# Mixer of a two-layer trunk: decay-weighted x made ahead of the scan, output transposes behind the next projection, B and C projected over all tokens at once

## The chip, the cores and the metric

The kernel runs on one core of a Trainium2 chip. The metric is the device time of one execution in microseconds (us); the kernel before has a median of 2000.05 us over three runs.

## The reference

Two layers, each of three sublayers on an x of 512 tokens by 1024 features, all in float32: a SwiGLU feed-forward, a mixer, a second feed-forward. Each sublayer reads a shifted and scaled x, its output is gated and added to x, and a layer norm follows. The change is in the mixer alone.

```python
h = modulate(x, shift, scale)
proj = h @ mix_w_in[l]                       # 1024 -> 3084
p_ssd, p_fox, p_sc = jnp.split(proj, ...)
y = jnp.concatenate([mamba2_group(p_ssd), fox_group(p_fox), shortconv_group(p_sc)]) @ mix_w_out[l]
x = layer_norm(ALPHA * x + gate * y)
```

The first group is a state space scan (SSD) with 8 heads of 64 features. Its projections are z, x, B and C; x, B and C go through a causal convolution of 4 taps and a SiLU. With dt a positive step for each token and head, a = -dt * A and cs the running sum of a inside a chunk, it computes

```python
y_diag = einsum(C B^T, exp(cs_i - cs_j), x * dt)         # inside a chunk
states = einsum(B, exp(cs_last - cs), x * dt)            # decay-weighted x: what a chunk leaves behind
y = y_diag + C @ (state carried in) * exp(cs) + D * x
y = rmsnorm(y * silu(z)) * norm_g                        # in two groups of 256 features
```

The second group is causal attention with a forgetting bias, 4 heads of 64, in four blocks of 128 queries (projections q, k, v). The third is B * conv3(C * x), from three projections of 256 features that the kernel calls SB, SC and SX.

## The kernel before

**Tiles.** The 512 tokens are four tiles of 128, one to a chunk of the scan (the kernel's chunk is 128 tokens) and one to a query block of the attention. The projections that the scan and the attention read by feature (B, C, x, q, k, SB, SC, SX) are made transposed: 128 features on the partitions, 512 tokens along the row. A call of feat (L761) makes 256 features, which are two PSUM banks of 128 features by 512 tokens.

**Exact products.** Each large product is three TensorE products (mm3): operands are split into a rounded high part and a remainder, and lo x hi, hi x lo and hi x hi are added up in PSUM. Names ending in h and l, or starting with them (hh, hl, hm, lm), are such pairs. Weights come by DMA from SyncE's queue in pieces of 128 x 2048; ScalarE makes the high part and VectorE subtracts it (the instructions named lm1z, lo, li and so on). The scan's small products, and the transposes with ident as the other operand, take plain float32.

**B and C.** feat has two switches for them. With halves=True a projection goes over tokens 0 to 255 for both banks and then over tokens 256 to 511, 8 k-steps of 3 products for each of the four quarters: 96 products 256 wide. All other calls of feat make 48 products 512 wide. With between=decays, the function decays (TensorE sums of a, the exponential edec, the attention's bias rows ncf) is called after the quarter that BPOS (L33) names, the third, and its first product is pinned behind that quarter's last one.

**The scan.** After x, B and C a loop over the four chunks transposes x back (pxt), and VectorE makes xdt = x * dt and xd = x * D from it. ssd_decay(i) makes the decay matrices: C B^T (pbc), masked by VectorE to cbm; the masked a (am, on GpSimd, L948), two TensorE products pd for each group, an exponential on ScalarE, and a VectorE product with cbm, which gives m. ssd_state(i) makes xw = xdt * edec in a temporary slot on VectorE, the products pss = B^T xw, and the new state. ssd_y(i) makes py = m xdt, eight products 64 wide, and adds it to xd; from chunk 1 on it adds the carried state's share. ssd_state is called for chunks 0 to 2 only, since nothing reads the state that the last chunk leaves. These steps stand between the projections of q, k and z.

**The end of the scan.** ssd_out(i) multiplies xd by the gate, takes the mean square of two groups with ScalarE, then a power of -1/2 on GpSimd (rs, L1001) and scales xd by it on VectorE (xd<-xd,rs). Then four TensorE transposes (pyt) turn the chunk to features by tokens; ScalarE evicts them with the norm's weight (yf) and makes the high part yh, and VectorE the remainder yl. These feed the output projection (po).

**The attention.** attn(i) makes qa, the split query, and then for each of four heads the scores (pS), their maximum (VectorE), the exponential (ScalarE), the scaled probabilities (prob), their transposes (pPT) and the products with the values (pfo).

**What sets the order.** The source is written in one order per step, and Tile's scheduler orders each engine's instructions from it by its own estimate; `after(ins, prev)` (it calls issue_after, L60) pins one instruction behind another on the same engine. Buffers come from pools: four PSUM banks in psa for projections, four in psb for everything else, 28 long-lived slots of 128 x 512 (slot), 9 temporary ones (tmp), 6 weight units. Engines are wrapped (InOrder, L43 to L56), so the profile gives L53 as the line of every recorded TensorE, VectorE and ScalarE instruction; which step it is can be read from its tile's name. At the end of the mixer the steps are called in the order attn(0), ssd_out(0), SC, attn(1), ssd_out(1), SX, attn(2), ssd_out(2), SB, attn(3), ssd_out(3), then the output projection.

Of the kernel before, what the change touches and what calls it, by code (L numbers as in the profile page):

```python
# [8 lines left out]
F32 = mybir.dt.float32  # L9
# [3 lines left out]
ALU = mybir.AluOpType  # L13
AX = mybir.AxisListType

P = 128
# [3 lines left out]
KD = D // P  # L20
# [9 lines left out]
NW = 6  # L30
PAD_W = 16
POS = 1
BPOS = 2  # L33
TICK = object()
CR = (2.7, 1.3)
WSZ = 1024
# [1 line left out]
C_Z, C_XS, C_B, C_C, C_DT = 0, 512, 1024, 1280, 1536  # L38
# [23 lines left out]
def issue_after(tc, ins, prev):  # L62

    tc.add_manual_dep(ins.ins, prev.ins.name,
                      mybir.DependencyInfo(mybir.DependencyClass.NoSync, mybir.DependencyReason.DATA),
                      reason="issue order")
# [3 lines left out]
def trunk(ctx, tc, x, c, ln_in_g, ln_in_b, ada_w, ada_b, ffn1_w_in, ffn1_w_out,  # L70
# [5 lines left out]
    pe, dve, act = (InOrder(tc, e) for e in (nc.tensor, nc.vector, nc.scalar))  # L76
# [18 lines left out]
    def pa(shape, name):  # L95
        return psa.tile(shape, F32, tag="a", name=name)

    def pb(shape, name):
        return psb.tile(shape, F32, tag="b", name=name)

    def slot(shape, dt, name):
        return lp.tile(shape, dt, tag="s", name=name)

    def tmp(shape, name, dt=F32):
        return tp.tile(shape, dt, tag="t", name=name)

    def mm3(ps, lh, ll, rh, rl, first, last):
        pe.matmul(ps, ll, rh, start=first, stop=False)
        pe.matmul(ps, lh, rl, start=False, stop=False)
        mm_last[0] = pe.matmul(ps, lh, rh, start=False, stop=last)  # L110

    mm_last = [None]

    def after(ins, prev):
        if prev is not None:
            issue_after(tc, ins, prev)


    ident = const.tile([P, P], F32, name="ident")
# [298 lines left out]
    def cols_unit(w, c0, name, prev=None):  # L418

        v = load(w, c0, 0, KD, 256, name)  # L420
        return [split(v[:, :, j * P:(j + 1) * P], f"{name}_{j}", prev) for j in range(2)]
# [6 lines left out]
    hT = [None, None]  # L428
# [203 lines left out]
    def x_affine(s, eng):  # L632

        ln_vectors(s)
        for t in range(NT):
            for h in range(2):
                xh = xt[t][:, h * 512:(h + 1) * 512]
                eng.tensor_tensor(xh, xh, aff[s, "g", h], ALU.mult)  # L638
                eng.tensor_tensor(xh, xh, aff[s, "b", h], ALU.add)
# [118 lines left out]
    def mixer(s, l):  # L758
        w_in, w_out = mix_w_in[l], mix_w_out[l]

        def feat(c0, name, epi, halves=False, between=None):  # L761

            us = cols_unit(w_in, c0, name)
            banks = [pa([P, T], f"pj{name}_{j}") for j in range(2)]
            for (a, b) in (((0, 256), (256, 512)) if halves else ((0, 512),)):
                for j in range(2):
                    wh, wl = us[j]
                    for k in range(KD):
                        mm3(banks[j][:, a:b], wh[:, k, :], wl[:, k, :],
                            hT[0][:, k, a:b], hT[1][:, k, a:b], k == 0, k == KD - 1)  # L770
                    if between is not None and (a > 0) * 2 + j == BPOS:
                        between(mm_last[0])
            for j in range(2):
                epi(j, banks[j])

# [2 lines left out]
        def conv_silu(ci, dst):  # L778
            def epi(j, ps):
                cc = ci + j  # L780
                w = lambda k: v_l[:, R_CW + k * 8 + cc:R_CW + k * 8 + cc + 1]
                acc = slot([P, T], F32, f"cv{s}_{cc}")
                act.activation(acc, ps, AF.Identity, scale=w(3), bias=v_l[:, R_CB + cc:R_CB + cc + 1])
                for sh in (1, 2, 3):
                    dve.scalar_tensor_tensor(acc[:, sh:], ps[:, :T - sh], w(3 - sh), acc[:, sh:],
                                             op0=ALU.mult, op1=ALU.add)
                silus.append(act.activation(acc, acc, AF.Silu))
                after(silus[-1], exp_done)
                dst[cc] = acc
            return epi  # L790

        xbc = {}
# [4 lines left out]
        us = []  # L797
# [8 lines left out]
        for t in range(NT):  # L806
            ts = slice(t * P, (t + 1) * P)
            ps = pa([P, 268], f"pv{s}_{t}")
            for k in range(KD):
                wh, wl = us[k // 3]  # L810
# [63 lines left out]
                dve.tensor_tensor(ncf[o:o + 4], psr[o:o + 4], ncf[o:o + 4].bitcast(F32), ALU.subtract)  # L874

        exp_done = edec = ncf = None
        feat(C_B, f"m{s}b", conv_silu(4, xbc), halves=True, between=decays)
        feat(C_C, f"m{s}c", conv_silu(6, xbc), halves=True)
        x_affine(s, pool)
        feat(C_XS, f"m{s}x0", conv_silu(0, xbc))  # L880
        feat(C_XS + 256, f"m{s}x1", conv_silu(2, xbc))
# [3 lines left out]
        for tt in range(2):  # L885
            ps = pb([P, 2, 2, P], f"pbt{s}_{tt}")
# [4 lines left out]
            b = slot([P, 2, 2, P], F32, f"btok{s}_{tt}")  # L891
# [1 line left out]
            btok.append(b)  # L893


        xdt, xd = [], []
        for t in range(NT):
            ts = slice(t * P, (t + 1) * P)
            ps = pb([P, 8, 64], f"pxt{s}_{t}")
            for cc in range(4):  # L900
                pe.transpose(ps[:, 2 * cc:2 * cc + 2, :], xbc[cc][:, ts], ident)
            if t % 2 == 0:
                xp = adap.tile([P, 2, 8, 64], F32, tag="ra", name=f"xdt{s}_{t}")
            a = xp[:, t % 2]
            b = slot([P, 8, 64], F32, f"xd{s}_{t}")
            dve.tensor_tensor(a, ps, dt8[:, t, :].unsqueeze(2).to_broadcast([P, 8, 64]), ALU.mult)
            dve.tensor_tensor(b, ps, dbc[l].unsqueeze(2).to_broadcast([P, 8, 64]), ALU.mult)
            xdt.append(a)
            xd.append(b)


        zs = []
# [45 lines left out]

        def ssd_state(i):

            xw = tmp([P, 8, 64], f"xw{s}_{i}")
            dve.tensor_tensor(xw, xdt[i], edec[:, 2, i, :].unsqueeze(2).to_broadcast([P, 8, 64]), ALU.mult)
            pss = pb([P, 8, 64], f"pss{s}_{i}")
            for g in range(2):
                pe.matmul(pss[:, 4 * g:4 * g + 4, :], btok[i // 2][:, i % 2, g, :],
                          xw[:, 4 * g:4 * g + 4, :], start=True, stop=True)
            snew = slot([P, 8, 64], F32, f"st{s}_{i}")
            if i == 0:
                act.activation(snew, pss, AF.Copy)
            else:  # L970
                dve.tensor_tensor(snew, state[i - 1], edec[:, 1, i, :].unsqueeze(2).to_broadcast([P, 8, 64]),
                                  ALU.mult)
                dve.tensor_tensor(snew, snew, pss, ALU.add)
            state.append(snew)
# [13 lines left out]
                dve.tensor_tensor(yo, pso, edec[:, 0, i, :].unsqueeze(2).to_broadcast([P, 8, 64]), ALU.mult)  # L988
                dve.tensor_tensor(xd[i], xd[i], yo, ALU.add)

        def ssd_out(i):
            y = xd[i].rearrange("p h d -> p (h d)")
            dve.tensor_tensor(y, y, zs[i], ALU.mult)
            ss = sm.tile([P, 2], F32, tag="ss", name="ss")
            sq = tmp([P, 512], "sq")
            for g in range(2):
                act.activation(sq[:, g * 256:(g + 1) * 256], y[:, g * 256:(g + 1) * 256], AF.Square,
                               scale=0.5, accum_out=ss[:, g:g + 1])
            dve.tensor_scalar(ss, ss, 1.0 / 256, RMS_EPS, op0=ALU.mult, op1=ALU.add)
            rs = sm.tile([P, 2], F32, tag="rs2", name="rs2")  # L1000
            pool.tensor_tensor(rs, ss, mhalf, ALU.pow)  # L1001
            for g in range(2):
                gs = slice(g * 256, (g + 1) * 256)
                dve.tensor_scalar(y[:, gs], y[:, gs], rs[:, g:g + 1], 0.5, op0=ALU.mult, op1=ALU.mult)
            ps = pb([P, 4, P], f"pyt{s}_{i}")
            for cc in range(4):
                pe.transpose(ps[:, cc, :], y[:, cc * P:(cc + 1) * P], ident)
            yf = slot([P, 4, P], F32, f"yf{s}_{i}")
            for cc in range(4):
                act.activation(yf[:, cc, :], ps[:, cc, :], AF.Copy, scale=v_l[:, R_NG + cc:R_NG + cc + 1])  # L1010
            yh = slot([P, 4, P], F32R, f"yh{s}_{i}")
            yl = slot([P, 4, P], F32R, f"yl{s}_{i}")
            act.activation(yh, yf, AF.Copy)
            dve.tensor_tensor(yl, yf, yh.bitcast(F32), ALU.subtract)
            yT.append((yh, yl))
# [110 lines left out]
        ssd_decay(0)  # L1126
        ssd_decay(1)
        ssd_state(0)
        ssd_y(0)
        feat(C_K, f"m{s}k", k_epi)  # L1130
        ssd_decay(2)
        ssd_state(1)
        ssd_y(1)
        z_proj()
        ssd_decay(3)
        ssd_state(2)
        ssd_y(2)
        ssd_y(3)
        attn(0)
        ssd_out(0)  # L1140
        feat(C_SC, f"m{s}sc", c_epi)
        attn(1)
        ssd_out(1)
        feat(C_SX, f"m{s}sx", x_epi)
        attn(2)
        ssd_out(2)
        feat(C_SB, f"m{s}sb", b_epi)
        attn(3)
        ssd_out(3)

        acts = [(lambda t, k=k: (yT[t][0][:, k, :], yT[t][1][:, k, :])) for k in range(4)]
        acts += [(lambda t, k=k: (fT[t][0][:, k, :], fT[t][1][:, k, :])) for k in range(2)]
# [6 lines left out]
    for s in range(6):  # L1159
        l, j = divmod(s, 3)  # L1160
# [39 lines left out]
```

## Time and profile before

| | us |
|---|---|
| median of three runs | 2000.05 |
| the three runs | 2003.78, 1996.82, 2000.05 |
| the profiled execution | 2000.76 |
| its span, first to last instruction | 1999.0 |
| mean granted TensorE clock | 0.995 |
| first mixer, from the B projection to the last attention block | about 416 to 616 |
| second mixer, the same stretch | about 1395 to 1595 |

The profiler took one execution. In its rows PE is TensorE's products, PEld its weight loads, DVE VectorE, ACT ScalarE, POOL GpSimd and SP SyncE. A row of the timeline gives start, duration, engine, line, operation, output<-inputs, shape and count; a bracket behind it is the engine's idle time just before, and the instruction that ended it. A row of the groups gives minimum/median/maximum or mean durations in ns and the first and last start. A row of the stages gives the stretch, its length, then each engine's busy time in the order PE, PEld, DVE, ACT, POOL, the granted clock, the DMA engines' busy share and GB/s. A row of the waits gives waiting tile, releasing tile, total us, count and longest. The second mixer's instructions lie about 979 us behind the first's and run in the same order.

### The profile page before, as it was taken

The numbers are of one execution on the slowest core, as the hardware profiler recorded it, in microseconds if no ns is written. First come the engines' busy times: TensorE is split into PE (matmuls) and PEld (weight loads), VectorE is DVE, ScalarE is ACT, GpSimd is POOL, SyncE is SP. The second block draws the span as 40 slices with busy tenths as digits, with TensorE's granted clock in tenths as the row PEclk, the third lists the DMA queues.
The fourth block names the chain that finished last, engine by engine and source line by source line (L and its number), as shares of the span: only waits on it lengthen the run. The fifth ranks groups of instructions, "written<-read, shape, count | busy, mean of one in ns | idle before, by whom it ended". The sixth has DMA issues, their size and how long they took to land.

```text
span 1999.0 us, 23434 instructions
## 1 busy us (share of the span) xinstructions
PE 1947.5 (97%) x9422; PEld 1627.3 (81%) x9422; DVE 1208.1 (60%) x1770; ACT 690.9 (35%) x1094; POOL 220.6 (11%) x182
## 2 busy tenths in 40 slices
PE   5999999999999999999999999999999999999998
PEld 4777878898878988888898788788978798888887
DVE  8886663477677655543477857435766785433336
ACT  3433223164365432123152322223544553222320
POOL 0230000007100040000005000000260004000000
PEclk9999999999999999999999999999999999999999
DMA  9766542234211544432345746232422144323331
GB/s 327 235 196 225 173 166 82 75 106 127 84 65 53 184 153 163 155 107 93 106 151 188 248 163 229 86 103 57 135 87 83 53 133 142 105 85 106 104 107 43
DMA packets 178605, 263.99 MB, mean 132 GB/s; under 512 B 9676, under 2 KB 124736, under 8 KB 178496
## 3 DMA queue, kind: packets, MB, share of 16 engines
q1 hardware_dynamic: 174000, 254.98, 38.8%
q10 hardware_dynamic: 4496, 7.52, 1.3%
q8 instruction: 74, 1.21, 0.2%
q14 instruction: 35, 0.29, 0.0%
HBM read 260.37 MB, written 2.10 MB: 131 GB/s over the span
## 4 chain that ended last, share of the span: by engine, by line
PE 77%; DVE 11%; DMA 7%; ACT 3%; issue 2%; POOL 0%; POOLq 0%; ACTq 0%; SPq 0%; DVEq 0%
PE pf L53 37%; PE po L53 23%; DMA ra<-in_ada_w_dram 6%; DVE acc L53 4%; PE pz L53 2%; DVE li L53 2%; DVE af L53 1%; PE pjm4x L53 1%; PE pjm1x L53 1%; PE ptr L53 1%; PE pS L53 1%; DMA ri<-in_ffn_w_in_dram 1%; PE py L53 1%; DVE x L53 1%; DVE gy L53 1%
## 5 line engine op out<-in xcount | busy, mean ns | idle before, releaser
L53 PE MATMUL pf<-hh,li 128*128 128x512 f32 (+1 forms) x1504 | 567.8, 378 | 1.4 <-DVE li L53 1.0
L53 PE MATMUL pf<-hl,hi 128*128 128x512 f32 (+1 forms) x1504 | 566.9, 377 | 0.2 <-DVE hl L53 0.2
L53 PE MATMUL pf<-hh,hi 128*128 128x512 f32 (+1 forms) x1504 | 566.9, 377 | 0.0
L53 DVE TENSOR_TENSOR li<-ri,hi 128x1024 fp32r<-128x1024 f32 x176 | 224.7, 1282 | 184.0 <-ACT hi L53 183.8
L53 PEld LDWEIGHTS pf<-hh,li 128*128 128x128 f32 x1504 | 284.4, 189 | 53.4 <-DVE li L53 1.7
L53 PEld LDWEIGHTS pf<-hl,hi 128*128 128x128 f32 x1504 | 284.2, 189 | 52.2 <-DVE hl L53 0.9
L53 PEld LDWEIGHTS pf<-hh,hi 128*128 128x128 f32 x1504 | 284.5, 189 | 51.3
L53 ACT ACTIVATE hi<-ri 128x1024 fp32r<-128x1024 f32 x176 | 185.5, 1060 | 311.1 <-PE pf L53 200.7
L53 PE MATMUL po<-ho,al 128*128 128x512 f32 (+1 forms) x704 | 273.5, 389 | 0.5 <-DVE af L53 0.4
L53 PE MATMUL po<-lo,ah 128*128 128x512 f32 (+1 forms) x704 | 272.9, 388 | 0.0
L53 PE MATMUL po<-ho,ah 128*128 128x512 f32 (+1 forms) x704 | 272.6, 388 | 0.0
L53 DVE TENSOR_TENSOR lo<-ro,ho 128x1024 fp32r<-128x1024 f32 x104 | 127.2, 1223 | 204.5 <-ACT ho L53 204.4
L53 DVE SCALAR_TENSOR_TENSOR acc<-ra,cT,acc 128x512 f32<-128x512 f32 x224 | 172.9, 815 | 67.1 <-DMA ra<-in_ada_w_dram 66.7
L53 ACT ACTIVATE ho<-ro 128x1024 fp32r<-128x1024 f32 x104 | 110.1, 1059 | 286.7 <-PE po L53 160.1
L451 POOL TENSOR_TENSOR rs<-ve,mhalf 128x1 f32<-128x1 f32 x28 | 17.3, 620 | 1277.5 <-DVE ve L53 1276.2
L53 PEld LDWEIGHTS po<-ho,al 128*128 128x128 f32 x704 | 132.2, 188 | 28.2 <-DVE af L53 0.8
L53 PEld LDWEIGHTS po<-ho,ah 128*128 128x128 f32 x704 | 132.2, 188 | 27.0
L53 PEld LDWEIGHTS po<-lo,ah 128*128 128x128 f32 x704 | 132.2, 188 | 26.9
L53 ACT ACTIVATE sg<-pf 128x512 f32<-128x512 f32 x88 | 52.4, 596 | 287.9 <-PE pf L53 270.7
L53 DVE TENSOR_TENSOR af<-sg,pf 128x512 f32<-128x512 f32 x88 | 60.1, 684 | 143.6 <-PE pf L53 141.0
L53 ACT ACTIVATE hf<-ptr,modB,modA 128x128 f32<-128x128 f32 (+1 forms) x168 | 67.0, 491 | 97.6 <-PE ptr L53 84.1
L638 POOL TENSOR_TENSOR x<-x,lng 128x512 f32<-128x512 f32 x48 | 75.5, 1598 | 218.7 <-DMA lng<-in_ln_g_dram 214.7
(397 smaller groups left out, 2488.3 us busy)
## 6 DMA issues: line engine op xcount, KB each, us to landing
ri<-in_ffn_w_in_dram SPq DMA_DIRECT2D x88, 1024.0 KB, 5.1
ra<-in_ada_w_dram SPq DMA_DIRECT2D x128, 512.0 KB, 3.9
ro<-in_ffn_w_out_dram SPq DMA_DIRECT2D x40, 1024.0 KB, 4.9
ro<-in_mix_w_out_dram SPq DMA_DIRECT2D x8, 1024.0 KB, 4.9
rf<-in_ada_w_dram SPq DMA_DIRECT2D x8, 512.0 KB, 8.4
ro<-in_ffn_w_out_dram SPq DMA_DIRECT2D x8, 512.0 KB
rf<-in_ada_w_dram SPq DMA_DIRECT2D x16, 192.0 KB, 6.5
gate<-in_ada_b_dram SPq DMA_DIRECT2D x12, 256.0 KB, 5.5
```

The lines of the kernel that those rows point to most:

```text
L53: ins = f(*a, **k)
L451: pool.tensor_tensor(rs, ve, mhalf[:, 0:1], ALU.pow)
L638: eng.tensor_tensor(xh, xh, aff[s, "g", h], ALU.mult)
```

## The change

It has three parts, all in the mixer.

1. feat loses halves and BPOS. B and C are made like the other projections, 48 products 512 wide each, and decays is called once all of B's products are issued.
2. xw is made in the loop that makes xdt and xd, for all four chunks, in long-lived slots; ssd_state only reads it.
3. ssd_out is divided into ssd_norm, all up to the scaled xd, and ssd_turn, from the transposes on. ssd_turn is called after the next projection, and its first transpose is pinned behind that projection's last product. Chunks 2 and 3 are normed one after the other ahead of SB, and turned one after the other behind it, ahead of attn(3).

```diff
-        def feat(c0, name, epi, halves=False, between=None):
+        def feat(c0, name, epi, between=None):
...
-            for (a, b) in (((0, 256), (256, 512)) if halves else ((0, 512),)):
-                for j in range(2):
-                    wh, wl = us[j]
-                    for k in range(KD):
-                        mm3(banks[j][:, a:b], wh[:, k, :], wl[:, k, :],
-                            hT[0][:, k, a:b], hT[1][:, k, a:b], k == 0, k == KD - 1)
-                    if between is not None and (a > 0) * 2 + j == BPOS:
-                        between(mm_last[0])
+            for j in range(2):
+                wh, wl = us[j]
+                for k in range(KD):
+                    mm3(banks[j], wh[:, k, :], wl[:, k, :], hT[0][:, k, :], hT[1][:, k, :], k == 0, k == KD - 1)
+            if between is not None:
+                between(mm_last[0])
...
-        feat(C_B, f"m{s}b", conv_silu(4, xbc), halves=True, between=decays)
-        feat(C_C, f"m{s}c", conv_silu(6, xbc), halves=True)
+        feat(C_B, f"m{s}b", conv_silu(4, xbc), between=decays)
+        feat(C_C, f"m{s}c", conv_silu(6, xbc))
...
             xdt.append(a)
             xd.append(b)
+            xw.append(slot([P, 8, 64], F32, f"xw{s}_{t}"))
+            dve.tensor_tensor(xw[t], a, edec[:, 2, t, :].unsqueeze(2).to_broadcast([P, 8, 64]), ALU.mult)
...
         def ssd_state(i):
 
-            xw = tmp([P, 8, 64], f"xw{s}_{i}")
-            dve.tensor_tensor(xw, xdt[i], edec[:, 2, i, :].unsqueeze(2).to_broadcast([P, 8, 64]), ALU.mult)
             pss = pb([P, 8, 64], f"pss{s}_{i}")
...
-        def ssd_out(i):
+        def ssd_norm(i):
...
+        def ssd_turn(i):
+            y = xd[i].rearrange("p h d -> p (h d)")
             ps = pb([P, 4, P], f"pyt{s}_{i}")
             for cc in range(4):
-                pe.transpose(ps[:, cc, :], y[:, cc * P:(cc + 1) * P], ident)
+                tr = pe.transpose(ps[:, cc, :], y[:, cc * P:(cc + 1) * P], ident)
+                if cc == 0:
+                    after(tr, mm_last[0])
...
         attn(0)
-        ssd_out(0)
+        ssd_norm(0)
         feat(C_SC, f"m{s}sc", c_epi)
+        ssd_turn(0)
         attn(1)
-        ssd_out(1)
+        ssd_norm(1)
         feat(C_SX, f"m{s}sx", x_epi)
+        ssd_turn(1)
         attn(2)
-        ssd_out(2)
+        ssd_norm(2)
+        ssd_norm(3)
         feat(C_SB, f"m{s}sb", b_epi)
+        ssd_turn(2)
+        ssd_turn(3)
         attn(3)
-        ssd_out(3)
```

The source does not tell how the scheduler merges these steps, so three places of the engines' orders are shown. The first is TensorE at the scan's first step, in the first mixer (pd the decay products, pss the state's, py the output's, pjm1k the key projection). Before:

```order
L53 MATMUL pd_1_1_3921<-am_1_1_0_3922,slowr 128x512
L53 MATMUL pjm1k_3958<-hh_2707,hm1k_3950 128x512
L53 MATMUL pd_1_1_3921<-am_1_1_1_3925,slowr 128x512
L53 MATMUL pjm1k_3958<-hh_2707,lm1k_3951 128x512
L53 MATMUL pjm1k_3958<-hl_2708,hm1k_3950 128x512
L53 MATMUL pjm1k_3958<-hh_2707,hm1k_3950 128x512
L53 MATMUL pjm1k_3958<-hh_2707,lm1k_3951 128x512
L53 MATMUL pss_0_3933<-xw_0_3931,btok_0_3772 128x256 x2
L53 MATMUL py_0_3938<-xdt_0_3786,m_0_0_3893 128x64 x4
L53 MATMUL py_0_3938<-xdt_0_3786,m_0_1_3903 128x64 x4
L53 MATMUL pjm1k_3958<-hl_2708,hm1k_3950 128x512
```

After:

```order
L52 MATMUL pd_1_1_3833<-am_1_1_0_3834,slowr 128x512
L52 MATMUL pss_0_3843<-xw_0_3694,btok_0_3676 128x256
L52 MATMUL pd_1_1_3833<-am_1_1_1_3837,slowr 128x512
L52 MATMUL pss_0_3843<-xw_0_3694,btok_0_3676 128x256
L52 MATMUL py_0_3848<-xdt_0_3690,m_0_0_3805 128x64 x4
L52 MATMUL py_0_3848<-xdt_0_3690,m_0_1_3815 128x64 x4
L52 MATMUL pjm1k_3868<-hh_2707,hm1k_3860 128x512
```

The two state products moved up between the decay products, and the key projection's five products that stood ahead of py went behind it.

The second place is VectorE over the same stretch (rows from the transposed x to the first m). Before:

```order
L53 TENSOR_TENSOR xdt_2_3803<-pxt_3_3807,dt 128x512
L53 TENSOR_TENSOR xd_3_3812<-pxt_3_3807,dbc_776 128x512
L53 TENSOR_TENSOR lm1z_0_4094<-rm1z_4091,hm1z_0_4093 128x1024
L53 TENSOR_TENSOR cbm<-pbc_0_3881,upper 128x256
L53 TENSOR_TENSOR lm1z_1_4098<-rm1z_4091,hm1z_1_4097 128x1024
L53 TENSOR_TENSOR cbm<-pbc_1_3906,upper 128x256
L53 TENSOR_TENSOR m_0_0_3893<-m_0_0_3893,cbm 128x512
L53 TENSOR_TENSOR m_0_1_3903<-m_0_1_3903,cbm 128x512
L53 TENSOR_TENSOR m_1_0_3918<-m_1_0_3918,cbm 128x512
L53 TENSOR_TENSOR xw_0_3931<-xdt_0_3786,edec 128x512
L53 TENSOR_TENSOR m_1_1_3928<-m_1_1_3928,cbm 128x512
```

After:

```order
L52 TENSOR_TENSOR xdt_2_3711<-pxt_3_3717,dt 128x512
L52 TENSOR_TENSOR xd_3_3722<-pxt_3_3717,dbc_776 128x512
L52 TENSOR_TENSOR xw_3_3725<-xdt_2_3711,edec 128x512
L52 TENSOR_TENSOR lm1z_0_4002<-rm1z_3999,hm1z_0_4001 128x1024
L52 TENSOR_TENSOR cbm<-pbc_0_3793,upper 128x256
L52 TENSOR_TENSOR lm1z_1_4006<-rm1z_3999,hm1z_1_4005 128x1024
L52 TENSOR_TENSOR cbm<-pbc_1_3818,upper 128x256
L52 TENSOR_TENSOR m_0_0_3805<-m_0_0_3805,cbm 128x512
L52 TENSOR_TENSOR m_0_1_3815<-m_0_1_3815,cbm 128x512
L52 TENSOR_TENSOR m_1_0_3830<-m_1_0_3830,cbm 128x512
L52 TENSOR_TENSOR m_1_1_3840<-m_1_1_3840,cbm 128x512
```

xw left its place between the third and the fourth m; each chunk's xw now stands right behind its xdt and xd, the last chunk's, which nothing reads, too.

The third place is TensorE from the end of the SB projection to the start of the output projection (pyt the scan's transposes, po the output projection, pS and pfo the attention). Before:

```order
L53 MATMUL po_0_0_0_5008<-ho_0_0_0_1_4994,yh_0_4379 128x512
L53 MATMUL pyt_2_4753<-ident,xd_2_3804 128x128 x4
L53 MATMUL pS_3_0_4845<-ka_0_4008,qa_3_4838 128x512
...
L53 MATMUL pfo_3_4837<-pth,vh_2_3271 128x256
L53 MATMUL pyt_3_4968<-ident,xd_3_3812 128x128 x4
L53 MATMUL po_0_0_1_5009<-lo_0_0_4_1_5005,gh_0_4828 128x512
```

After:

```order
L52 MATMUL pjm1sb_4680<-hl_2708,hm1sb_4675 128x512
L52 MATMUL pjm1sb_4680<-hh_2707,hm1sb_4675 128x512
L52 MATMUL pyt_2_4739<-ident,xd_2_3712 128x128 x4
L52 MATMUL pyt_3_4753<-ident,xd_3_3722 128x128 x2
L52 MATMUL po_0_0_0_4914<-ho_0_0_0_0_4896,yl_0_4350 128x512
L52 MATMUL pyt_3_4753<-ident,xd_3_3722 128x128 x2
L52 MATMUL po_0_0_0_4914<-lo_0_0_0_0_4897,yh_0_4349 128x512
```

Chunk 2 is turned behind SB's last product as before the last attention block, and chunk 3 is turned right with it, where before it came after that block's last product.

More of the change, by code (lines that the diff above doesn't have):

```diff
@@ L32 @@
 POS = 1
-BPOS = 2
 TICK = object()
@@ L893, in mixer @@
             btok.append(b)
-        xdt, xd = [], []
+        xdt, xd, xw = [], [], []
         for t in range(NT):
@@ L965, in ssd_state @@
                 pe.matmul(pss[:, 4 * g:4 * g + 4, :], btok[i // 2][:, i % 2, g, :],
-                          xw[:, 4 * g:4 * g + 4, :], start=True, stop=True)
+                          xw[i][:, 4 * g:4 * g + 4, :], start=True, stop=True)
             snew = slot([P, 8, 64], F32, f"st{s}_{i}")
```

## The prediction

> **What bounds the kernel now.** I read the page's busy times first, then its chain, then the busy times by stage, then TensorE's waits in the first of the two mixers.
>
> ```profile
> span 1999.0 us, 23434 instructions
> PE 1947.5 (97%) x9422; PEld 1627.3 (81%) x9422; DVE 1208.1 (60%) x1770; ACT 690.9 (35%) x1094; POOL 220.6 (11%) x182
> PE 77%; DVE 11%; DMA 7%; ACT 3%; issue 2%; POOL 0%; POOLq 0%; ACTq 0%; SPq 0%; DVEq 0%
> 416.00:491.00 75.00, 74.83 (x493) 68.30 (x492) 55.67 (x92) 39.28 (x65) 32.00 (x23) 1.00 0.45 139
> 491.00:536.00 45.00, 42.89 (x209) 35.62 (x208) 26.57 (x31) 21.25 (x33) 13.32 (x11) 1.00 0.20 59
> 536.00:616.00 80.00, 78.47 (x422) 61.96 (x421) 60.09 (x142) 42.48 (x112) 2.78 (x4) 1.00 0.24 79
> PE pss L53 <- DVE xw L53: 2.1, 2, 1.4
> PE pyt L53 <- DVE xd L53: 1.2, 3, 0.4
> ```
>
> TensorE is busy for 97% of the span, at a granted clock of 1.00 in these stages, with the DMA engines at 0.20 to 0.45. So the change pays in only two ways: TensorE does the same products in less time, or it loses a wait. The stage rows read span, PE, PEld, DVE, ACT, POOL: in the 200 us that the change touches, TensorE idles 0.17, 2.11 and 1.53 us. The two wait rows name nearly all of that: 2.1 us for xw, 1.2 us for the scaled y ahead of its transposes. The second mixer repeats the first to 0.1 us, so each term below is worked out once and doubled. If all of both waits went, that would be 6.6 us of 1999.
>
> The profiled execution took 2000.76 us, its span 1999.0; the median of the runs is 2000.05. I make the sum against 2000.76 and take off 0.7 at the end. A measurement of this kernel can tell about 0.3%, here 6.0 us, from no change.
>
> **B and C over all tokens.** The next rows are the C projection, 96 products 256 wide, and the x projection, 96 products 512 wide: first and last start stand behind the durations.
>
> ```profile
> L53 PE MATMUL pjm1c<-hh,lm1c x32: 283/283/283, 443.2 to 454.4; 128*128 128x256 f32 x32
> L53 PE MATMUL pjm1c<-hh,hm1c x32: 283/283/283, 443.5 to 454.6; 128*128 128x256 f32 x32
> L53 PE MATMUL pjm1x<-hh,lm1x x32: 389/389/396, 454.7 to 475.8; 128*128 128x512 f32 x32
> L53 PE MATMUL pjm1x<-hh,hm1x x32: 389/389/393, 455.2 to 476.3; 128*128 128x512 f32 x32
> ```
>
> The durations overlap, so the rate is read from the starts: 11.4 us over 95 steps is 120 ns for a narrow product, 21.6 over 95 is 227 ns for a wide one. One wide for two narrow saves 13 ns; 96 such pairs a mixer save 1.2 us, **2.4 us** in all. The Trainium skill (TensorE: Matmul & The Clock Gate, section Back-to-back issue gap) gives an isolated gap of N/2.4 + 2.5 ns; an estimate from it is 109 and 216 ns, 2.5 ns a pair and 0.5 us in all. The trace has 13 ns, and I go by it; by the page the sum would be 1.9 us smaller.
>
> The cover that the halves gave is not needed: the first B product already stands among the last V products, which read the same last tokens. The decay sums now come after all of B. They are 2 us later; the first to read them is xw, some 40 us on.
>
> **xw ahead of the scan.** These are TensorE's rows around the two stalls, with the tile's own row last.
>
> ```profile
> 498.05 0.40 PE L53 MATMUL pjm1k<-hh,lm1k 128*128 128x512 f32 x1
> 499.20 1.13 PE L53 MATMUL pss<-xw,btok 128*128 128x256 f32 x4 [0.75 <-DVE xw L53]
> 501.87 0.48 PE L53 MATMUL pjm1k<-hl,hm1k 128*128 128x512 f32 x1
> 502.19 0.39 PE L53 MATMUL pjm1k<-hh,hm1k 128*128 128x512 f32 x1
> 514.05 0.39 PE L53 MATMUL pz<-hm1z,hl 128*128 128x512 f32 x1
> 515.80 1.13 PE L53 MATMUL pss<-xw,btok 128*128 128x256 f32 x4 [1.36 <-DVE xw L53]
> L53 DVE TENSOR_TENSOR xw<-xdt,edec x6: 683/1522/1528, 497.6 to 1519.7; 128x512 f32<-128x512 f32 x6
> ```
>
> From start to start the stalls cost 1.15 and 1.75 us where a product takes 0.23: 0.92 + 1.52 = 2.44 a mixer, 4.9 in all, if xw is ready. It will be, 10 us early. Against that, the new order puts each state product singly between two decay products, so three times a mixer TensorE leaves the full-precision products once more; 501.87 to 502.19 is 0.32, not 0.23, so 3 x 0.09 x 2 = 0.5 us.
>
> What xw may delay is the other half of the same step. Its four multiplies (one more than before: the last chunk's is never read) now stand ahead of cbm and m, which the y products read. Here are VectorE and, in the last two rows, GpSimd there.
>
> ```profile
> 484.42 0.67 DVE L53 TENSOR_TENSOR xdt<-pxt,dt 128x512 f32<-128x512 f32 x1
> 491.11 0.42 DVE L53 TENSOR_TENSOR cbm<-pbc,upper 128x256 f32<-128x256 f32 x1 [2.77 <-PE pbc L53]
> 492.30 1.89 DVE L53 TENSOR_TENSOR lm1z<-rm1z,hm1z 128x1024 fp32r<-128x1024 f32 x1 [0.77 <-ACT hm1z L53]
> 494.54 0.42 DVE L53 TENSOR_TENSOR cbm<-pbc,upper 128x256 f32<-128x256 f32 x1 [0.34 <-PE pbc L53]
> 494.93 2.76 DVE L53 TENSOR_TENSOR m<-m,cbm 128x512 f32<-128x512 f32 x3
> 483.23 1.03 POOL L948 TENSOR_TENSOR am<-a12h,upper 128x512 fp32r<-128x512 f32 x1
> 487.23 2.02 POOL L948 TENSOR_TENSOR am<-a12h,upper 128x512 fp32r<-128x512 f32 x1
> ```
>
> VectorE has 2.77 + 0.77 + 0.34 = 3.9 us to spare there. Four xw take 2.7 us at 683 ns and 6.1 us at 1522 ns, so they overrun it by 0 to 2.2. The two m that y needs were done after two thirds of the m row, at 496.8; in the new order five products fewer stand ahead of y, so TensorE reaches it at 498.28 - 5 x 0.23 and some 0.9 for the state products, 498.0 of the old time, which takes off another 1.2. So the new wait is 0 to 1.0 us a mixer. GpSimd works during most of the stretch, which speaks for 1522, and stops near 489, which speaks for less; I take 0.3, **0.6 us** for both. The later steps have their m before TensorE comes to y. Net: 4.9 - 0.5 - 0.6 = **3.8 us**.
>
> **The transposes behind the next projection.** The first four rows are VectorE around chunk 1's norm, the next three TensorE at chunk 0's transposes, the last chunk 1's; chunk 3's wait is the rest of the 1.2 above, 0.40.
>
> ```profile
> 573.21 0.17 DVE L53 TENSOR_SCALAR ss<-ss 128x2 f32<-128x2 f32 x1
> 574.19 0.61 DVE L53 TENSOR_SCALAR xd<-xd,rs 128x256 f32<-128x256 f32 x2 [0.81 <-POOL rs L1001]
> 574.84 0.42 DVE L53 TENSOR_TENSOR qa<-q,qa 64x256 fp32r<-64x256 f32 x1
> 576.19 0.69 DVE L53 TENSOR_TENSOR sc<-pjm1sx,sc 128x512 f32<-128x512 f32 x1
> 558.91 0.40 PE L53 MATMUL pjm1sx<-hl,hm1sx 128*128 128x512 f32 x1
> 559.68 0.63 PE L53 MATMUL pyt<-ident,xd 128*128 128x128 f32 x4 [0.37 <-DVE xd L53]
> 560.71 0.36 PE L53 MATMUL pS<-ka,qa 128*128 128x256 f32 x1
> 574.69 0.63 PE L53 MATMUL pyt<-ident,xd 128*128 128x128 f32 x4 [0.44 <-DVE xd L53]
> ```
>
> VectorE stands still for 0.81 us at every norm, waiting for GpSimd, and whatever is queued behind it (qa, so the next scores) is late by as much. The pin to the projection's last product moves less than the words say, since the projections were already interleaved with the attention:
>
> Chunk 0: one product more ahead of the transposes (0.23), one fewer between them and the scores, which wait for qa behind the same norm. Old 0.37, new 0.37.
>
> Chunk 1: eleven products, 2.5 us, now stand between the last attention product and the transposes, so 0.44 goes. But VectorE now does the short convolution's steps and sc, which needs the projection's last product, ahead of qa. From that end sc and qa take about 0.45 + 0.69 + 0.42 = 1.6 us, while TensorE has 0.44 of transposes and 4 products, 1.35. With VectorE late from the norm I take a new 0.3.
>
> Chunks 2 and 3: two norms in a row on VectorE and eight transposes in a row on TensorE. From chunk 2 scaled to chunk 3 scaled is 0.17 + 0.81 + 0.35 = 1.33 us, less 0.44 for the first four transposes: 0.9, and 0.2 for the second half, which has an eviction ahead of it. Old 0.40, new 1.1. The scores after it wait another 0.1 for qa.
>
> Sum: old 1.21, new 1.87, a loss of 0.66 a mixer, **1.3 us**. The bounds are a gain of 1.2 a mixer (nothing new) and a loss of about 2 (each late item also late for the next).
>
> **The end of the output projection.** The new order finishes the first half's four outputs within its last 12 products instead of one after another. So VectorE begins their folds later.
>
> ```profile
> 628.39 0.68 DVE L53 BATCH_NORM_STATS2 st<-x 128x6 f32<-128x512 f32 x1
> 629.00 1.21 DVE L53 TENSOR_TENSOR li<-ri,hi 128x1024 fp32r<-128x1024 f32 x1
> 630.12 0.69 DVE L53 TENSOR_TENSOR gy<-po,gate 128x512 f32<-128x512 f32 x1
> 633.37 0.81 DVE L53 TENSOR_SCALAR x<-x,mv,rs 128x1024 f32<-128x1024 f32 x1 [0.67 <-POOL rs L451]
> 635.38 1.04 PE L53 MATMUL ptr<-ident,x 128*128 128x128 f32 x8
> ```
>
> Twelve folds 0.61 apart and one split of 1.2 are 8.5 us from 1.65 before the half's end, then 4.1 (630.12 to 634.2): 10.9 after it, when TensorE has done 48 products of 0.227, also 10.9. The old spare 1.2 is gone; I take 0.1 a mixer, **0.2 us**.
>
> Sum: 2.4 + 3.8 - 1.3 - 0.2 = 4.7 us. 2000.76 - 4.7 = 1996.1, on the median's scale **1995.4 us**, 0.24% faster: within 0.3%.
>
> **The rivals.** *Everything is collected.* No m waits, and the three transposes' waits go with none in their place: 2.4 + 4.9 - 0.5 + 2.4 = 9.2, 1990.9 us. For it: the planner that ordered the instructions left hardly any other wait in this stage. Against it: the 0.81 us of GpSimd stays in VectorE's queue. 0.27.
>
> *xw's stall changes its place.* VectorE and GpSimd stretch each other (683 against 1522 ns, 1.03 against 2.02), all four xw run long, and TensorE waits 1.0 for m at the first step and as much again because GpSimd's am come later for the second: 4.0 us given back instead of 0.6. The sum is 1.3, 1998.8 us. The Trainium skill (SBUF — State Buffer, section SBUF: two separate sides) speaks for this: the port pair shared by the two engines is an exclusive lock for whole instructions with two SBUF inputs. The trace agrees for xw, and its 0.67 for xdt, which reads PSUM while GpSimd is busy, shows such an operation untouched. Against it: only part of the stretch has GpSimd busy. 0.13.
>
> *VectorE paces the attention.* At 60.1 of 80 us it is the next engine there, and the new order puts the convolution and two norms ahead of the maxima.
>
> ```profile
> 592.27 1.23 DVE L53 TENSOR_TENSOR lo<-ro,ho 128x1024 fp32r<-128x1024 f32 x1 [0.34 <-ACT ho L53]
> ```
>
> If in the last two attention blocks each pair of heads waits for one such split, that is 4 x 1.23 x 2 = 9.8 us in place of the 1.3: a sum of -3.8, 2003.9 us, slower. It decides from three such waits a mixer on, where 7.4 passes the 6.0 that the rest brings. Against it: of TensorE's waits in the old mixer none is for probabilities. 0.10.
>
> **How the numbers follow.** The forecast has 0.50. Its own range is 1993.3 (no new cost: 2.4 + 4.4 = 6.8) to 1998.5 (m at its bound and 1.5 a mixer lost at the transposes: 4.7 - 1.4 - 1.7 = 1.6). Faster by over 0.3% means under 1994.0: a quarter of the forecast, since the runs shown lie from 1996.8 to 2003.8 and their median may be off by a us, 0.13, and the first rival, 0.27: 0.40. Slower by over 0.3% is over 2006: a good third of the last rival, 0.04, and 0.02 for what I have not seen: 0.06. The rest is 0.54. The range goes from the first rival with a us to spare, 1989.8, to 2001.0, which leaves out most of the third.
>
> **What would show it.** Right: B and C at 227 ns a product, no wait of TensorE for xw, a wait of about 1 us at chunk 3's transposes, some tenths at the scores of blocks 1 and 2. Wrong: TensorE waiting for m at the y products (second rival); 3 us or more of waits for prob or qa a mixer (third); fewer than 0.5 us of waits a mixer between 536 and 616 (first).

## The result, and the profile after

The changed kernel takes 1989.81 us (median of four runs, 1988.98 to 1990.74) against 1999.34 for the kernel before (four runs): ratio 0.995, interval 0.9931 to 0.9969. That is 9.5 us faster, where 4.7 were forecast; the number is near the first rival's 9.2. In six more runs beside eleven of before it was 0.9947 (0.9928 to 0.9967).

The head of the page and three stage rows (columns as in the prediction) of the changed kernel:

```profile
span 1988.4 us, 23091 instructions
PE 1940.2 (98%) x9230; PEld 1615.1 (81%) x9230; DVE 1210.2 (61%) x1772; ACT 689.0 (35%) x1094; POOL 220.8 (11%) x182
416.00:489.00 73.00, 72.82 (x390) 62.41 (x389) 57.98 (x96) 38.64 (x63) 33.07 (x23) 1.00 0.45 141
489.00:532.00 43.00, 43.00 (x213) 36.39 (x213) 25.99 (x31) 21.49 (x33) 13.63 (x11) 1.00 0.20 62
532.00:612.00 80.00, 78.21 (x423) 62.11 (x422) 62.14 (x144) 45.96 (x118) 2.79 (x4) 1.00 0.24 81
```

The scan's stage (second of the three) has lost its 2.11 us of idle TensorE and holds none now. The attention's stage idles 1.79 us, where it was 1.53. The waits of TensorE in the first mixer say which instructions wait:

```profile
PE pS L52 <- DVE qa L52: 0.7, 1, 0.7
PE pyt L52 <- DVE xd L52: 0.7, 1, 0.7
PE pv L52 <- DVE hl L52: 0.2, 1, 0.2
PE pS L52 <- ACT fhl L52: 0.2, 1, 0.2
```

xw is gone from the list. Two new waits stand in the attention, both of VectorE's making. Here they are on TensorE, with chunk 1's transposes, which wait no longer:

```profile
569.99 0.60 PE L52 MATMUL pyt<-ident,xd 128*128 128x128 f32 x4
572.26 0.41 PE L52 MATMUL pS<-ka,qa 128*128 128x384 f32 x1 [0.73 <-DVE qa L52]
588.43 0.60 PE L52 MATMUL pyt<-ident,xd 128*128 128x128 f32 x4
589.72 0.41 PE L52 MATMUL pyt<-ident,xd 128*128 128x128 f32 x2 [0.69 <-DVE xd L52]
```

To set kernels against each other I take from each trace the stretch from the first V product's start to the last output product's start, in both mixers, and call what is left of the span the rest. In the first mixer before, that is from 416.3 us on; its first B product starts at 428.2. Before, the mixers are 231.48 and 231.48 us; after, 227.30 and 227.32. So the mixers hold 4.18 + 4.16 = 8.3 us. The rest went from 1536.0 to 1533.8, though no instruction of it was touched.

### The profile page after: what moved, and what is told of

Its sections match the earlier page's. It is cut to its first block, busy times and chain, and to the rows that moved or that the text cites. A ratio compares the mean times of both kernels' runs of the same rounds, so it can differ in the third digit from the quotient of the medians.

```text
span 1988.4 us, 23091 instructions
## 1 busy us (share of the span) xinstructions
PE 1940.2 (98%) x9230; PEld 1615.1 (81%) x9230; DVE 1210.2 (61%) x1772; ACT 689.0 (35%) x1094; POOL 220.8 (11%) x182
## 4 chain that ended last, share of the span: by engine, by line
PE 83%; DVE 8%; DMA 5%; ACT 3%; issue 1%; POOL 0%; SPq 0%; POOLq 0%; DVEq 0%; ACTq 0%
PE pf L52 40%; PE po L52 25%; DMA ra<-in_ada_w_dram 4%; DVE acc L52 3%; PE pz L52 2%; PE pjm4x L52 1%; PE pjm1x L52 1%; DVE af L52 1%; DVE li L52 1%; PE pS L52 1%; PE ptr L52 1%; PE py L52 1%; ACT hf L52 1%; PE pfo L52 1%; DVE x L52 1%
```

## The experiments

Where the table gives no ratio, the kernel was executed once.

| | mixers, us | rest, us | ratio to before (interval) |
|---|---|---|---|
| before | 231.48, 231.48 | 1536.0 | 1 |
| the change | 227.30, 227.32 | 1533.8 | 0.9950 (0.9931 to 0.9969) |
| E1 before again | 231.54, 231.48 | 1530.1 | 0.9993 (0.9983 to 1.0004) |
| E2 wide B and C only | 230.32, 230.36 | 1538.2 | 0.9981 (0.9970 to 0.9993) |
| E3 xw only | 228.44, 229.51 | 1531.7 | 0.9958 (0.9943 to 0.9973) |
| E4 third part only | 232.19, 232.12 | 1536.1 | 0.9999 (0.9989 to 1.0009) |
| E5 the change without the third part | 227.24, 227.21 | 1538.0 | |
| E6 the change, xw twice | 227.48, 227.38 | 1532.6 | |
| E7 the change, chunk 3 turned late | 228.06, 228.05 | 1535.6 | |
| E8 the change, query first | 225.95, 225.91 | 1538.2 | |
| E9 the change again | 227.33, 227.38 | 1534.9 | 0.9947 (0.9928 to 0.9967) |
| E10 query first again, timed | 226.00, 226.16 | 1530.5 | 0.9943 (0.9923 to 0.9963) |
| E11 query first, no third part | 228.76, 228.91 | 1531.3 | |
| E12 query first, chunk 3 late | 226.22, 226.18 | 1532.6 | |

**E1, the kernel before again.** No edit.

> The kernel before once more, unchanged. The two profiles differ by 10.6 us of span, of which the mixers' own stretches (first V product to last output product: 231.5 us each before, 227.3 each after) hold only 8.3; 2.3 lie in the feed-forwards and the start, where the change touches no instruction. Theory A: those 2.3 us are scatter of one execution against another (waits for the adaLN vectors, a few us at half the pace). Then this run has its mixers at 231.5 us each within 0.2, but the rest of its span off the 1536.0 us of the first profile of before by about 1 to 2 us, and a ratio of 1.000. Theory B: they belong to the change. Then the rest is 1536.0 within 0.5 here, and each run of a part below shows a part of the 2.3.

The mixers came back to 0.06 us. The rest came out 5.9 us shorter than in the first profile of the same kernel, far more than theory A had put at 1 to 2. Over all kernels it lies between 1530.1 and 1538.2; E8 and E10 are one kernel, and theirs differ by 7.7. All of that scatter lies in the stretches ahead of each mixer: from the second mixer's end on, the 14 profiles have 372.05 to 372.07 us, while the first mixer begins at 413.9 to 420.2 and 743.6 to 749.5 lie between the two. So a mixer's stretch tells tenths of a microsecond from one profile, and the time of a whole execution does not.

**E2, E3, E4: each part alone**, on the kernel before. The edits are the change's own lines: feat and its two calls; the xw lines of the xdt loop and of ssd_state; ssd_norm, ssd_turn and the call order.

> Only the B and C projections over all tokens, all else as before. Both theories (A: each part is worth what its own place in the profile shows; the forecast on record) say 13 ns for each of 96 pairs a mixer: the two projections' stretch 1.2 us shorter, each mixer 230.3 us, 2.4 us in all, ratio 0.9988. Against them: without the halves the first C products wait for the convolution or the decay sums that now come later, mixers 231 us or more.

1.16 and 1.12 us a mixer, as said.

> Only xw made ahead of the scan. Theory A: no wait takes the place of the two stalls of xw and leaving the full-precision products costs nothing; each mixer is 2.65 us shorter, 228.8 us, 5.3 in all, ratio 0.9974. The forecast on record: 0.25 us a mixer for the switches and 0.3 for m, 1.9 shorter, 229.6 us, 3.8 in all, ratio 0.9981, with a wait of TensorE for m at the first y products.

3.04 us in the first mixer. The second's 1.97 holds 1.29 us of waiting at a V product, ahead of anything that the part touches. TensorE never waits for m. Both theories were low: 2.64 of the 3.04 lie in the scan, up to the end of the z projection, and 0.40 behind it. The times gained more than the mixers: the ratio is 8.4 us of 2000, and its interval ends at 0.9973, just short of the 0.9975 that the mixers' 5.0 us would make.

> Only the scan's end divided, with the transposes behind the next projection. Theory A: the waits of TensorE grow as forecast (1.2 to about 1.6 us a mixer by the list of waits), but the output projection and the scores are interrupted less, which gives back more: each mixer 0.3 us shorter, 231.2 us, 0.6 in all, ratio 0.9997. The forecast on record: 0.66 us longer, 232.1 us, 1.3 slower in all, ratio 1.0007. If the parts do not add up, for instance when this part is worth more alone than with xw ahead of the scan, the mixer is off 231.2 by over 0.3.

0.71 and 0.64 us longer: alone, the third part costs what the forecast said, and theory A, which I had read from the changed kernel, falls. The lists of waits of E4's attention and of the end of its output projection:

```profile
PE pyt L53 <- DVE xd L53: 1.3, 3, 0.7
PE pS L53 <- DVE qa L53: 0.3, 1, 0.3
PE ptr L53 <- DVE x L53: 0.7, 1, 0.7
```

The 0.7 at ptr, the transposes of the finished x, is as large as the whole loss. The other waits rose too, from 1.2 to 1.6, and that was made good in rows that show no wait. So the size came out by luck, as two misses cancel: the waits that were to cost 0.66 cost nothing, and the end of the output projection cost 0.7 where 0.1 was said. The next two rows are E4's VectorE as its folds begin, the two behind them the changed kernel's at the same place.

```profile
623.01 1.23 DVE L53 TENSOR_TENSOR li<-ri,hi 128x1024 fp32r<-128x1024 f32 x1 [2.88 <-ACT hi L53]
624.27 1.29 DVE L53 TENSOR_TENSOR gy<-po,gate 128x512 f32<-128x512 f32 x2
```

```profile
615.76 1.23 DVE L52 TENSOR_TENSOR li<-ri,hi 128x1024 fp32r<-128x1024 f32 x1 [3.97 <-ACT hi L52]
618.07 1.37 DVE L52 TENSOR_TENSOR gy<-po,gate 128x512 f32<-128x512 f32 x2 [1.08 <-PE po L52]
```

In E4 a weight split (li) stands right ahead of the folds, waits 2.88 us for ScalarE, and the folds begin the moment it ends. In the changed kernel the split is done earlier, and VectorE waits 1.08 us for TensorE: the folds begin as soon as the bank is finished, and ptr never waits. That the split makes the wait is read from these rows; no run moved it alone. E11 below has a split in the same place and 0.6 at ptr, but in E7 one ends right ahead of the folds and ptr does not wait.

**E5, the change without its third part.** Parts 1 and 2 on the kernel before.

> The change without its third part: B and C over all tokens and xw ahead of the scan, the scan's end as before. The parts alone gave, each mixer: B and C 1.15 us shorter, xw 3.04 (its first mixer; the second holds a wait of 1.29 us at a V product that no other run has), the third part 0.68 longer; they sum to 3.5, the whole change gave 4.17. Theory A: the third part's price depends on what stands around it and is 0.0 on top of the other two, so each mixer is 231.48 - 1.15 - 3.04 = 227.3 us here. Theory B: the third part costs its 0.68 in the whole change too and the other two help each other: 226.6 us.

227.24 and 227.21: theory A. The first two parts alone make the whole gain of the mixers, and the third is worth 0.0 on top of them (0.1 longer with it, if anything), though alone it cost 0.68. Its price depends on what stands around it. By the rows of E4 that is where the scheduler puts a weight split at the other end of the stage, which is argued and not shown.

**E6, xw twice**, on the changed kernel.

```diff
-            dve.tensor_tensor(xw[t], a, edec[:, 2, t, :].unsqueeze(2).to_broadcast([P, 8, 64]), ALU.mult)
+            for _ in range(2):
+                dve.tensor_tensor(xw[t], a, edec[:, 2, t, :].unsqueeze(2).to_broadcast([P, 8, 64]), ALU.mult)
```

> The changed kernel with each of the four xw computed twice (the second writes the same values again): the cost that the forecast feared, doubled. Theory A: the four xw fit in VectorE's idle time with little to spare. The second m was done at 495.44 us and TensorE reached y at 496.34, 0.9 of room; 0.76 of VectorE's idle time is left ahead of the two m (0.42 and 0.34). Four more xw take two times 0.60 and two times 1.25, 3.7 us, so TensorE waits 3.7 - 0.9 - 0.8 = 2.0 us for m at the first y products of each mixer: 229.3 us a mixer. Theory B: m was never near the path (TensorE would do other products first, or VectorE has more room): under 0.5 us of wait, 227.3 to 227.8 us.

No wait for m, 0.18 and 0.06 us longer: theory A of this run falls, and with it the forecast's fear. The first row is VectorE's four m in E6, the second TensorE's first y products there.

```profile
492.91 4.68 DVE L52 TENSOR_TENSOR m<-m,cbm 128x512 f32<-128x512 f32 x4
495.82 1.45 PE L52 MATMUL py<-xdt,m 128*128 128x64 f32 x12
```

Even with eight xw ahead of them the four m start at 492.91, and half of their 4.68 us is over at 495.3, before y begins at 495.82. Two things had been left out. The first four heads' products need only the first m, and the second m is due 0.8 us later. And VectorE's rows ahead of m stretch and shrink with what GpSimd does meanwhile, so four more multiplies did not make it later by their sum.

TensorE's order was not the same, though: 21 key products stand ahead of y in E6, 17 in the changed kernel. Counted from the first V product, E6's first two m were done at 79.64 and 81.09 us (78.07 and 79.52 in the changed kernel), and y began at 81.36. Had y begun at the changed kernel's 80.41 with m as late as here, its first half would still have found the first m, and its second half, at 81.25, the second. So the room was there, with under 0.2 us to spare, and the order added to it.

**E7, chunk 3 turned behind the last attention block**, on the changed kernel.

```diff
-        ssd_turn(3)
         attn(3)
+        ssd_turn(3)
```

> The changed kernel with chunk 3's transposes back behind the last attention block, its norm still ahead of the SB projection. Theory A: the second half of the double norm (0.69 us of wait, 0.85 by the steps) and the eviction between the transposes (0.1) are off TensorE's path: each mixer 0.9 us shorter, 226.4 us. Theory B: the gain is taken back, by the output projection's order (four outputs that finish in another sequence, folds later on VectorE) or by more interruptions of it: 227.3 us or more.

0.75 us longer in each mixer: theory B, by another way than it said. The 0.69 us of wait at chunk 3's transposes is gone, and the last block's scores wait for qa instead; TensorE's row, then VectorE's row for qa and the one ahead of it:

```profile
596.59 0.47 PE L52 MATMUL pS<-ka,qa 128*128 128x512 f32 x1 [0.97 <-DVE qa L52]
```

```profile
595.30 0.69 DVE L52 TENSOR_TENSOR su<-pjm1sb,su 128x512 f32<-128x512 f32 x1
596.02 0.87 DVE L52 TENSOR_TENSOR qa<-q,qa 64x256 fp32r<-64x256 f32 x2
```

qa reads nothing that is new; it waits its turn on VectorE behind two norms and the short convolution's last step. That holds for the 0.73 us of the changed kernel too, which is what the next run removes.

**E8 and E10, each block's query split first**, on the changed kernel. The split of the query leaves attn for a function of its own, called ahead of the norm.

```diff
         attn(1)
+        split_q(2)
         ssd_norm(1)
...
         attn(2)
+        split_q(3)
         ssd_norm(2)
```

> The changed kernel with the split of each block's query (qa, qb) called ahead of the norm and the projection's last step that it stood behind on VectorE. Theory A: the wait of TensorE for qa (0.73, 1.17 by the steps) goes and nothing takes its place, since the transposes of chunk 1 had 2.5 us of projection ahead of them: each mixer 1.0 us shorter, 226.3 us. Theory B: the norm is later by the two qa (0.9 us) and the transposes of chunks 0 and 3 wait for it by as much instead: 227.3 us within 0.3.

1.35 and 1.41 us shorter a mixer, theory A and a little more. The waits of E8's first mixer in the attention:

```profile
PE pyt L52 <- DVE xd L52: 0.8, 2, 0.6
```

1.6 us of waits at qa, pyt and the attention's result (fhl) became 0.8. This is the shortest mixer of the study.

> The changed kernel with each block's query split ahead of the norm, timed. Its profile had each mixer at 225.9 us, 1.37 shorter than the changed kernel. Theory A: 11.1 us less than before in all, ratio 0.9945, and 2.7 us under the changed kernel's time of this same comparison (about 0.0014 of ratio, near what the intervals can tell). Against it: the gain in the profile does not show in the times, same ratio as the changed kernel.

The mixers again had 226.0 and 226.2. The times can't tell 2.7 us: medians 1987.1 and 1989.0, ratios 0.9943 and 0.9947 with intervals of 0.002 to each side. The gain stands in the profiles, and is not shown in the times.

**E9, the change again.** No edit.

> The changed kernel once more, unchanged, against the kernel before in more runs. The mixers hold 8.35 us of the gain and the rest of the span went from 1530.1 to 1538.2 us in the profiles so far, whatever the kernel. Theory A: all of the change's gain is in the mixers, so the ratio settles near 1 - 8.35/2000 = 0.9958 and the rest of this profile lies anywhere between 1530 and 1538. Theory B: the change also makes the rest shorter by about 2 us: ratio 0.9950 or less.

0.9947, and 0.9958 lies inside its interval, as it does inside the first one. Both medians lean to theory B by a microsecond or two; with a rest that scatters by 8 us, this stays open.

**E11, query first without the third part**, on E5's kernel, with split_q(i + 1) ahead of ssd_out(i).

> The query split ahead of the norm as in the run before, but with the scan's end as in the kernel before (norm and transposes together, behind their own attention block); B and C and xw as in the change. Theory A: the third part, worth 0.0 with qa behind the norm, is what lets qa go first: here the norm is later by the two qa and the transposes stand right behind it, so the three waits at the transposes (1.0 us together) grow and the gain of 1.37 does not come: 227.0 to 228.5 us a mixer. Theory B: moving qa alone brings the gain, the third part is needless: 226.2 us or less.

```profile
PE pyt L53 <- DVE xd L53: 2.4, 4, 0.8
PE ptr L53 <- DVE x L53: 0.6, 1, 0.6
```

228.8 and 228.9, theory A and a little past its upper end: the waits at the transposes grew from 1.0 to 2.4 us. So the third part is worth nothing on top of the other two and 2.9 us a mixer (228.8 less 225.9) once the query goes first: it puts other products between the norm and the transposes, and only then does the norm have time to give away.

**E12, query first and chunk 3 late.**

> The changed kernel with the query split ahead of the norm and chunk 3's transposes behind the last attention block. Chunk 3 late alone lost 0.75 us a mixer, of which the new wait of TensorE for qa (0.97, 1.36 by the step) ahead of the last block is the largest item. Theory A: with qa out of the way that wait cannot come, and the double transposes' wait is gone already, so this is equal to the query split alone, 225.9 us a mixer within 0.3. Theory B: chunk 3 late loses by the end of the output projection (order of its four outputs), so it loses here too, 226.4 us or more.

226.2 and 226.2, theory A: without qa behind the norms, chunk 3's place changes at most 0.3 us.

## Right and wrong, point by point

**The sum.** For both mixers together, B and C were put at 2.4 us and gave 2.3; xw at 3.8, and gave 6.1 (E3's first mixer, doubled); the transposes and the end of the output projection at a loss of 1.5, and cost 0.2 (the change against E5). So 4.7 became 8.3. Two steps failed: the charges of 1.1 set against xw's stalls, of which nothing came, and the price of the third part, added up from new waits. Another 1.2 us of xw's gain was in no term. What the times show beyond the mixers, 1.2 of the 9.5 us, stays open.

**What bounds it: right.** All of the mixers' gain is less time for the same products or a lost wait, and the second mixer repeated the first.

**B and C: right.** 1.2 a mixer said, 1.16 and 1.12 measured. The first row is B before (x is in the prediction), the next two are B and x after; from B's first start to x's first start is all of B and C.

```profile
L53 PE MATMUL pjm1b<-hh,lm1b x32: 278/283/365, 428.2 to 442.9; 128*128 128x256 f32 x32
```

```profile
L52 PE MATMUL pjm1b<-hh,lm1b x16: 389/389/400, 427.7 to 439.5; 128*128 128x512 f32 x16
L52 PE MATMUL pjm1x<-hh,lm1x x32: 389/389/389, 453.1 to 474.2; 128*128 128x512 f32 x32
```

Before, 454.7 less 428.2 is 26.5; after, 453.1 less 427.7 is 25.4. The Trainium skill (TensorE: Matmul & The Clock Gate, section Back-to-back issue gap) adds 2.5 ns to a product on its own, an estimate of 0.24 us a mixer. This stream of products, each with a weight load of its own, gave 1.1, and the measurement decides.

**xw: right in its mechanism, too low in size.** The stalls were worth their 2.44 a mixer. The two charges against them were not there. The first, 0.25 for leaving the full-precision products more often, failed in its working: it took the slow step behind a switch (0.32 for 0.23) without the quick step ahead of it. The changed kernel shows the pair:

```profile
495.01 0.40 PE L52 MATMUL pd<-am,slowr 128*128 128x512 f32 x1
495.25 0.59 PE L52 MATMUL pss<-xw,btok 128*128 128x256 f32 x2
495.49 0.58 PE L52 MATMUL pd<-am,slowr 128*128 128x512 f32 x1
495.91 0.59 PE L52 MATMUL pss<-xw,btok 128*128 128x256 f32 x2
496.34 1.89 PE L52 MATMUL py<-xdt,m 128*128 128x64 f32 x16
```

From the first row to y is 1.33 us for two decay and four state products. Before, y began at

```profile
500.17 1.89 PE L53 MATMUL py<-xdt,m 128*128 128x64 f32 x16
```

so four state products alone took 0.97 (499.20 to 500.17), and two decay products are 0.46: single or in a row, they cost the same. The second charge, 0.3 for m, failed because VectorE had room, as E6 shows. Here are VectorE's xw and what stands behind them, then GpSimd beside them:

```profile
480.55 0.68 DVE L52 TENSOR_TENSOR xw<-xdt,edec 128x512 f32<-128x512 f32 x1
482.35 0.68 DVE L52 TENSOR_TENSOR xw<-xdt,edec 128x512 f32<-128x512 f32 x1
484.14 1.33 DVE L52 TENSOR_TENSOR xw<-xdt,edec 128x512 f32<-128x512 f32 x1
486.60 1.32 DVE L52 TENSOR_TENSOR xw<-xdt,edec 128x512 f32<-128x512 f32 x1
493.29 2.76 DVE L52 TENSOR_TENSOR m<-m,cbm 128x512 f32<-128x512 f32 x3
```

```profile
482.34 1.58 POOL L947 TENSOR_TENSOR am<-a12h,upper 128x512 fp32r<-128x512 f32 x1
483.89 1.04 POOL L947 TENSOR_TENSOR am<-a12l,upper 128x512 fp32r<-128x512 f32 x1
484.89 1.49 POOL L947 TENSOR_TENSOR am<-a12h,upper 128x512 fp32r<-128x512 f32 x1
```

The four took 4.0 us, between the bounds of 2.7 and 6.1. At each overlap one of the two engines is stretched and the other is not: at 482.35 xw keeps its 0.68 and am takes 1.58, at 484.14 am keeps its 1.04 and xw takes 1.33. The Trainium skill's exclusive lock (SBUF — State Buffer, section SBUF: two separate sides), which goes to the instruction that starts first, fits that at 484.14; at 482.35 the two starts are 0.01 us apart, too close to tell. The stretching did not become the second rival, since TensorE waited for none of the stretched ones. Beyond the stalls xw alone brought 0.2 a mixer in the scan and 0.40 behind the z projection, where the waits at the transposes fell only from 1.2 to 1.0 and a new one of 0.2 came, of the output projection for yl. What made that was not separated.

**The transposes: the items near, the sum wrong.** Chunk 3's double norm was put at 0.9 and a new wait for qa, behind chunk 1's norm, at 0.3; they are 0.69 and 0.73 in the list of waits, and the waits together went from 1.2 to 1.6, where 1.9 was forecast. The loss of 0.66 a mixer still did not come: E5 puts the third part at 0.0 on top of the others. The step that failed is that the waits made up the sum. From the z projection's last product to the last output product the same products took 111.8 us before, 111.5 in E5 and 111.5 after. The 0.3 is thus gained without the third part. That part adds 0.4 of waits to E5's 1.2, and as much was saved in rows that show no wait. How is not shown: TensorE leaves the output projection for other products 15 times in that stretch before, and 12 times in E5 as well as after, so fewer interruptions do not tell the third part apart.

**The end of the output projection: mis-sized, and in the wrong kernel.** 0.1 a mixer was said. It is 0.7 in E4 and nothing in the changed kernel, by the place of one weight split as far as the rows tell.

**The rivals.** The first one's number came near, 9.2 said and 8.3 in the mixers, but by luck: it took 2.4 us from the transposes, which gave nothing, and 4.4 from xw, which gave 6.1. The waits that were to go rose from 1.2 to 1.6 a mixer. The second and third are refuted: no wait for m, none for prob.

**The pin.** Without `after(tr, mm_last[0])` the scheduler puts every engine's instructions in the same order, so the third part is its call order alone.

## What to carry to other kernels

Where one engine is 97% busy, take a stall's price from the waits, but let a new order's price come from a run: here the same edit cost 0.68 us a mixer, nothing, or gained 2.9, by what stood beside it in another engine's queue. Ask of every instruction that TensorE waits for whether it reads anything new; qa did not, and calling it one step earlier, with the transposes moved as well, was worth as much as a third of the whole change. Compare a stage's stretch between traces when the whole time scatters more than the edit is worth.

## What the runs showed of the hardware

The scatter of the rest comes in part from TensorE's clock. These are the kernel before, TensorE around a wait in a feed-forward, and then two stretches of it with the granted clock (the third column from the end):

```profile
1133.30 0.78 PE L53 MATMUL pm<-gh,onesr 128*128 128x512 f32 x1 [2.12 <-ACT gh L53]
1134.31 0.63 PE L53 MATMUL pm<-gh,onesr 128*128 128x512 f32 x1
1134.74 0.63 PE L53 MATMUL pm<-gl,onesr 128*128 128x512 f32 x1
```

```profile
1133.50:1136.50 3.00, 3.00 (x8) 2.19 (x9) 2.75 (x5) 1.07 (x2) 0.00 (x0) 0.50 0.72 216
1137.00:1142.00 5.00, 5.00 (x23) 4.14 (x23) 4.30 (x9) 1.55 (x2) 0.00 (x0) 1.00 0.77 235
```

After 2.12 us of waiting the clock was 0.50 for some 3 us, and products started 0.43 us apart where 0.23 is usual. From 1133.30 to 1136.83 eight steps from start to start took 3.53 us instead of 1.84, a cost of about 1.7. In E7 it happened after 1.50 us:

```profile
1132.46 0.50 PE L52 MATMUL pm<-gh,onesr 128*128 128x512 f32 x1 [1.50 <-ACT gh L52]
1132.50:1136.50 4.00, 4.00 (x10) 2.71 (x11) 3.64 (x7) 1.23 (x2) 0.00 (x0) 0.64 0.75 231
```

In the changed kernel's profile 2.35 us of waiting at the same place had nothing of the kind behind it. The Trainium skill (TensorE: Matmul & The Clock Gate, section Part 1: The HAM clock gate) puts the half clock behind an idle window of about 3.4 us. These waits are shorter, so here the measurement decides against that figure. E8's profile has four such stretches between 130 and 1260 us and that of E10, the same kernel, two; at 1.7 each that is up to 3.4 of the 7.7 us between their rests. The mixers' stalls of 1.36 us showed no such stretch in any run, so the change did not save any there.
